# Two projections of a gated MLP as seven products of block sums, in a pass of their own

## The chip, the cores and the metric

The kernel runs on one core of a Trainium2 chip. The metric is the device time of one execution, in microseconds (us), the median of the runs of one kernel. A core has a matrix engine (PE), three engines for elementwise work (DVE, the vector engine; ACT, the activation engine; POOL, GpSimd), and SP, whose queue here issues most DMA transfers. Each engine works through its own queue in order and waits at an instruction whose inputs are not there yet.

## The reference

One encoder layer over 4096 tokens of width 1024, in fp32. All column groups are slices of one projection of the normalised input:

```python
h = rms_norm(x, norm_g[layer])
proj = h @ w_in[layer]
q, k, v, g_att, sg_uv, g_sg, q_mem, g_mem = jnp.split(proj, split_points, axis=-1)
...
uv = jax.nn.gelu(sg_uv)
u, vv = jnp.split(uv, 2, axis=-1)
vv = layer_norm(vv, sg_ln_g[layer], sg_ln_b[layer])
vv = vv.reshape(B, S // SG_CHUNK, SG_CHUNK, N_SG_GROUPS, SG_GROUP_DIM)
mixed = jnp.einsum('gpq,bcqge->bcpge', sg_w[layer], vv)
mixed = mixed + jnp.transpose(sg_b[layer])[None, None, :, :, None]
y_sg = (u * mixed.reshape(B, S, SG_WIDTH)) * jax.nn.silu(g_sg)
```

Here u is columns 2048 to 2559 of the projection, vv 2560 to 3071 and the gate g_sg 3072 to 3583, 512 each. Beside this group stand a dilated attention (q, k, v) and an attention into 256 memory tokens (q_mem, mem); the three results go through one output projection, a residual and a final norm.

## The kernel before

An fp32 product is made of three fp32r matmuls: both factors are split into a high part (a cast on ACT) and the rest (a subtraction on DVE), and high x high, high x low and low x high are summed in PSUM (`mm3`, L194 to L201). One 128 x 1024 by 1024 x 512 product is a group of 8 k-tiles x 3 = 24 matmuls of 128x512.

Raw blocks of 256 KB come from HBM through five buffers (`raw`), for x (`load_x_kt`, L182: cast L185 to `xh`, subtraction L186 to `xl`) and for weights (`load_w_kt`, L165: scaled cast L168 to `wh`, L169 to `wl`, the norm's gain g folded in). Weights lie in three slots of eight pairs: slot 0 in the pool px, slots 1 and 2 in the pool pw. x has ten pairs of buffers, so two k-tiles of the next 512 tokens can be made ready early. The tokens' norm factor rs is not applied to x but to the result (as the scale of an activation, or in a multiplication).

`pass_a` (0 to 575 us) makes v, q and k for eight tiles T of 512 tokens. In its last T it loads vv's weights into slot 0. `pass_b` (575 to 1130 us) makes for each T, in four groups each, vv (slot 0, W[0]), u (slot 1, W[1]) and the gate (slot 2, W[2]). vv passes through Gelu (ACT, L359), statistics, a reciprocal root (POOL, L109) and two scalings (DVE, L361 to L367), and is split again (cast L368, subtraction L369). Then `pm` mixes the positions of a 128-token chunk: 24 matmuls of 128x256 (L392 to L395 call `mm3`), read by L400, which adds a bias and multiplies with u times its gate; L401 stores the result. After pass_b come the memory's keys (L471) and values (L484), q_mem with its gate, the attention and the output projection.

What sets the order: a scheduler places the instructions of each engine by data dependence and estimated times, up to the last T of pass_b; from there on PE, ACT and DVE run in the order in which the code is written (`manual_schedule`, L349).

## Time and profile before

| | us |
|---|---|
| median of three runs | 3117.7 (3115.72 to 3122.05) |
| the profiled execution | 3116.74 |
| its span on the core | 3115.0 |
| PE busy in the span | 3026.7 (97%) |
| pass_b in the trace | 575.27 to 1130.40 |

The span runs from the first to the last instruction of the profiled execution. Busy times of several engines overlap. Matmuls of PE are pipelined: a record lasts about 0.39 us while the next starts 0.23 us after it, so a rate is read from a window and its count. PEclk is the granted clock of PE as a share of its full speed, 2.4 GHz; 0.50 is 1.2 GHz.

### The profile page before, as it was taken

The page shows a single profiled execution, that of the slowest core. Times are in us where ns is not written, and L with a number is a line of the kernel's source. Part 1 is how long each engine was busy: PE and PEld are TensorE (multiplying, and loading weights), DVE is VectorE, ACT ScalarE, POOL GpSimd, SP SyncE. Part 2 cuts the span into 40 slices and gives each one's busy share as a digit, 9 for nine tenths or more (in the row PEclk, how much of TensorE's full clock was granted, in tenths as well). Part 3 has the DMA queues.
Part 4 walks back from the last instruction along what each step waited for, and adds up shares of the span by engine and source line. Part 5 has one row for each costly group of instructions (what it writes and reads, how often), then busy time and mean ns, then how long its engine had stood idle before and what let it go on. Part 6 is the DMA issues. An engine that isn't in the chain of part 4 may idle for free. (4 is left out here: it accounts for less than half of the span.)

```text
span 3115.0 us, 44121 instructions
## 1 busy us (share of the span) xinstructions
PE 3026.7 (97%) x15850; PEld 2526.2 (81%) x15850; DVE 1414.3 (45%) x3669; ACT 1235.0 (40%) x2504; POOL 365.1 (12%) x708
## 2 busy tenths in 40 slices
PE   9999999999999999999999988999999988999998
PEld 7777888888888888888887877888888876888887
DVE  4332323433333355565553345555665564444443
ACT  5213111322222245554553346677766742111111
POOL 1111112000000000000000011122122211111120
PEclk9999999999999999999999999999999998999999
DMA  8558445411211152121127466767777478778773
GB/s 284 189 173 260 155 136 173 145 41 43 66 55 41 36 174 72 51 78 48 51 72 223 152 140 158 147 142 157 158 169 148 106 188 224 200 198 202 207 191 100
DMA packets 344067, 432.47 MB, mean 139 GB/s; under 512 B 154179, under 2 KB 230302, under 8 KB 334630
## 3 DMA queue, kind: packets, MB, share of 16 engines
q1 hardware_dynamic: 325832, 387.26, 45.3%
q0 software_dynamic: 17440, 41.33, 5.2%
q8 instruction: 126, 2.06, 0.3%
q10 hardware_dynamic: 576, 1.05, 0.1%
q14 instruction: 93, 0.76, 0.1%
HBM read 299.27 MB, written 130.21 MB: 138 GB/s over the span
## 5 line engine op out<-in xcount | busy, mean ns | idle before, releaser
L199 PE MATMUL acc<-xh,wh 128*128 128x512 f32 x1192 | 473.6, 398 | 11.1 <-ACT xh L185 11.1
L200 PE MATMUL acc<-xl,wh 128*128 128x512 f32 x1192 | 471.7, 396 | 10.5 <-DVE xl L186 10.3
L201 PE MATMUL acc<-xh,wl 128*128 128x512 f32 x1192 | 470.4, 395 | 0.0
L199 PE MATMUL acc<-wh,xh 128*128 128x512 f32 x1024 | 401.1, 392 | 0.0
L200 PE MATMUL acc<-wl,xh 128*128 128x512 f32 x1024 | 401.0, 392 | 0.0
L201 PE MATMUL acc<-wh,xl 128*128 128x512 f32 x1024 | 400.9, 392 | 0.0
L756 ACT ACTIVATE p<-ring,negm 128x256 f32<-128x256 f32 (+1 forms) x768 | 330.7, 478 | 166.7 <-DVE negm L743 166.7
L667 DVE CUSTOM_DVE_ANT_0 ring<-s,tab 128x256 f32<-128x256 f32 (+1 forms) x768 | 272.3, 392 | 108.9 <-PE s L662 87.7
L200 PEld LDWEIGHTS acc<-xl,wh 128*128 128x128 f32 x1192 | 226.0, 190 | 64.8 <-DVE xl L186 16.8
L199 PEld LDWEIGHTS acc<-xh,wh 128*128 128x128 f32 x1192 | 226.0, 190 | 64.6 <-ACT xh L185 14.9
L201 PEld LDWEIGHTS acc<-xh,wl 128*128 128x128 f32 x1192 | 226.1, 190 | 48.1
L809 PE MATMUL o<-ph,vt 128*65 128x256 f32 (+1 forms) x1280 | 246.5, 340 | 10.7 <-DMA vt<-v 10.7
L662 PE MATMUL s<-khh,qs 128*128 128x256 f32 (+1 forms) x768 | 228.1, 321 | 0.0
L201 PEld LDWEIGHTS acc<-wh,xl 128*128 128x128 f32 x1024 | 191.9, 187 | 43.8
L199 PEld LDWEIGHTS acc<-wh,xh 128*128 128x128 f32 x1024 | 191.9, 187 | 43.4
L200 PEld LDWEIGHTS acc<-wl,xh 128*128 128x128 f32 x1024 | 191.9, 187 | 43.4
L185 ACT CAST xh<-raw 128x512 fp32r<-128x512 f32 x256 | 153.1, 620 | 182.6 <-DMA raw<-in_xT_s 106.5
L809 PEld LDWEIGHTS o<-ph,vt 128*65 128x65 f32 x1280 | 166.5, 139 | 72.5 <-issue 13.5
L825 DVE COPY oacc<-o 65x512 f32<-65x512 f32 x192 | 132.2, 689 | 204.7 <-PE o L809 142.0
L186 DVE TENSOR_TENSOR xl<-raw,xh 128x512 fp32r<-128x512 f32 x256 | 167.6, 687 | 94.8 <-ACT xh L185 93.4
L1133 PE MATMUL acc<-w,aa 128*128 128x512 f32 x768 | 193.3, 401 | 13.5 <-ACT aa L1118 8.3
L662 PE MATMUL s<-kll,qs 128*128 128x256 f32 (+1 forms) x768 | 198.3, 282 | 0.0
(238 smaller groups left out, 4697.0 us busy)
## 6 DMA issues: line engine op xcount, KB each, us to landing
raw<-in_xT_s SPq DMA_DIRECT2D x256, 256.0 KB
og<-oD SPq DMA_DIRECT2D x16, 1536.0 KB
w3k<-wD SPq DMA_DIRECT2D x32, 768.0 KB
oD<-oacc POOLq DMA_DIRECT2D x46, 512.0 KB, 4.7
raw<-in_w_in SPq DMA_DIRECT2D x72, 256.0 KB
xn<-in_x_s SPq DMA_DIRECT2D x32, 512.0 KB
v<-t POOLq DMA_DIRECT2D x128, 128.0 KB, 5.3
khh<-kH SPq DMA_DIRECT2D x32, 512.0 KB
```

Of the source, the lines that this page charges most:

```text
L185: nc.scalar.copy(h[:, :n], raw[:, :n])
L186: nc.vector.tensor_sub(lo[:, :n], raw[:, :n], f(h[:, :n]))
L199: nc.tensor.matmul(out, lh, rh, start=i == 0, stop=False)
L200: nc.tensor.matmul(out, lh, rl, start=False, stop=False)
L201: nc.tensor.matmul(out, ll, rh, start=False, stop=i == n - 1)
L662: nc.tensor.matmul(ps[:, b1, :B["n"]], q, kv, start=i == 0, stop=i == 1)
L667: self.last_dve = nc.vector.tensor_tensor_reduce(out=ring[:, bi, :n], in0=ps[:, b1, :n], in1=e["tab"][:, c, 64 * B["o"]:64 * B["o"] + n], ...
L756: nc.scalar.activation(out, in_, AF.Exp, bias=e["negm"][:, bi:bi + 1], scale=1.0)
L809: nc.tensor.matmul(o[:, o0:o1], vt[:, t, :], pT[:, c0:c1], start=t == 0, stop=t == 4, skip_group_check=True)
L825: nc.vector.tensor_copy(dst, o)
L1133: nc.tensor.matmul(ps, l, w, start=a, stop=o, skip_group_check=True)
```

## The change

u and its gate leave pass_b. A new `pass_u` between pass_a and pass_b treats 256 tokens at a time (16 steps r). With A the 256 x 1024 block of rs times x, cut into four blocks (two token halves of 128, two k halves of 512), and B the 1024 x 1024 weights of u and gate, cut likewise, it forms seven products of 128 x 512 by 512 x 512, 12 matmuls each, in place of eight: A11·B11, S2·T2, S1·T1, S3·T3, A12·B21, A22·T4 and S4·B22. S1 to S4 are sums of blocks of A, T1 to T4 of B. Three PSUM banks per step take them; between products DVE adds the parts that two results share (p1, u2, u3).

- Weights: `split_parts`, called three times in the last T of pass_a, in place of the load of vv's weights, makes T1 to T4, B11, B21 and B22 (40 raw blocks, 12 differences on POOL). B11 and T2 go to slot 0, T1 and T3 to slot 1 (Wq's buffers, free after the last q group), B21 and T4 to slot 2 (Wk's, free after the last k group), B22 into a new pool pz. Vv's weights are loaded in the last step of pass_u.
- `prep(r)`, written one step ahead: one DMA of 1 MB for x (two buffers), the product with rs on POOL (128x2048), four sums on POOL (128x512), seven casts on ACT, seven subtractions on DVE.
- After the products: five adds and two products on DVE, a copy, two Gelu and two Silu on ACT; the 256 x 512 result (u times gate) goes to HBM (`ug`), and pass_b loads it per T (1 MB).
- pass_b: its u and gate groups and their weights' loads are gone; `u` has two buffers; Wmv is loaded one T earlier.

```diff
@@ pass_a, last T
-                    self.Wvv = self.load_w(0, self.w_in(2560), self.g_in)
+                    self.split_parts(0)
...
+                        if T == NT - 1 and cb == 3:
+                            self.split_parts(1 if W is Wq else 2)
...
+    def split_parts(self, rnd):
...
+        def put(name, slot, src, g, kt):
+            pool = (self.px, self.pw, self.pw, self.pz)[slot]
...
+            if g is None:
+                nc.scalar.copy(h, src)
+                nc.vector.tensor_sub(lo, src, f(h))
+            else:
+                nc.scalar.activation(h, src, AF.Copy, scale=g)
+                nc.vector.scalar_tensor_tensor(lo, src, g, f(h), ALU.mult, ALU.subtract)
+
+        def tmp():
+            return self.pz.tile([P, 512], F32, name="wt", tag="wt", bufs=2)
+
+        for kt in range(4):
+            g1, g2 = g_[:, kt:kt + 1], g_[:, kt + 4:kt + 5]
+            b11, b12, b22 = raw(0, 0, kt), raw(0, 1, kt), raw(1, 1, kt)
...
+            if rnd != 1:
+                d, t2 = tmp(), tmp()
+                nc.gpsimd.tensor_sub(d, b12, b11)
+                nc.scalar.activation(d, d, AF.Copy, scale=g1)
+                nc.vector.scalar_tensor_tensor(t2, b22, g2, d, ALU.mult, ALU.subtract)
...
+            else:
+                b21 = raw(1, 0, kt)
+                put("B21", 2, b21, g2, kt)
+                nc.vector.scalar_tensor_tensor(t2, b21, g2, t2, ALU.mult, ALU.subtract)
+                put("T4", 2, t2, None, kt)
+
+    def pass_u(self):
...
+            def prep(r):
...
+                x = p.tile([P, KT, NI], F32, name="xr", bufs=2)
+                nc.sync.dma_start(x, a["xT_s"][:, r * NI:(r + 1) * NI].rearrange("(k p) t -> p k t", p=P))
...
+                nc.gpsimd.tensor_mul(x, x, rs)
+                a11, a12, a21, a22 = [x[:, 4 * j:4 * j + 4, P * i:P * (i + 1)] for i in range(2) for j in range(2)]
+                s1, s2, s3, s4 = [p.tile([P, 4, P], F32, name="s%d" % i, bufs=1) for i in range(4)]
...
+                put("A11", a11)
+                nc.gpsimd.tensor_add(s1, a21, a22)
+                nc.gpsimd.tensor_sub(s2, s1, a11)
+                put("S2", s2)
+                put("S1", s1)
+                nc.gpsimd.tensor_sub(s3, a11, a21)
+                put("S3", s3)
+                put("A12", a12)
+                put("A22", a22)
+                nc.gpsimd.tensor_sub(s4, a12, s2)
+                put("S4", s4)
...
+            for r in range(2 * NT):
...
+                product(b1, "A11", "B11", True)
+                nc.scalar.copy(p1, b1)
+                product(b2, "S2", "T2", True)
+                nc.vector.tensor_add(u2, b2, p1)
+                product(b3, "S1", "T1", True)
+                product(b2, "S3", "T3", False)
+                nc.vector.tensor_add(u3, b2, p1)
+                product(b1, "A12", "B21", False)
+                nc.vector.tensor_add(c22, b3, u3)
+                product(b2, "A22", "T4", False)
+                product(b3, "S4", "B22", False)
+                if r < 2 * NT - 1:
+                    X = prep(r + 1)
+                else:
+                    self.Wvv = self.load_w(0, self.w_in(2560), self.g_in)
+                nc.vector.tensor_add(w[:, 1], b2, p1)
+                nc.vector.tensor_add(c12, b3, u2)
+                nc.scalar.activation(w[:, 0], b1, AF.Gelu_apprx_tanh)
+                nc.scalar.activation(w[:, 1], w[:, 1], AF.Gelu_apprx_tanh)
+                nc.scalar.activation(c22, c22, AF.Silu)
+                nc.scalar.activation(c12, c12, AF.Silu)
+                nc.vector.tensor_mul(w[:, 0], w[:, 0], c12)
+                nc.vector.tensor_mul(w[:, 1], w[:, 1], c22)
+                nc.sync.dma_start(self.ug[r * NI:(r + 1) * NI, :].rearrange("(j p) c -> p j c", p=P), w)
...
@@ pass_b
-                u = p.tile([P, 4, 512], F32, name="u", tag="u")
+                u = p.tile([P, 4, 512], F32, name="u", tag="u", bufs=2)
+                nc.sync.dma_start(u, self.ug[T * TT:(T + 1) * TT, :].rearrange("(j p) c -> p j c", p=P))
...
-                if T == 0:
-                    W[1] = self.load_w(1, self.w_in(2048), self.g_in)
-                    W[2] = self.load_w(2, self.w_in(3072), self.g_in)
-                for j in range(4):
...
-                    self.proj_N(ps, W[1], X, j)
-                    nc.scalar.activation(u[:, j, :], ps, AF.Gelu_apprx_tanh, scale=rs)
-                if T == NT - 1:
+                if T == NT - 2:
                     self.Wmv = self.load_w(1, a["w_kv"][:, 512:1024], self.g_mem)
-                for j in range(4):
...
-                    self.proj_N(ps, W[2], X, j)
-                    t = p.tile([P, 512], F32, name="t", tag="t1", bufs=3)
-                    nc.scalar.activation(t, ps, AF.Silu, scale=rs)
-                    nc.vector.tensor_mul(u[:, j, :], u[:, j, :], t)
```

Three places show how the order of the instructions moves. In all of them a number behind a name is that of the buffer's use. **SP at the end of pass_a**, before: the stores of the last k blocks (kH, kL), the last x block and four of vv's weight blocks.

```order
L308 DMA kH<-qkh 128x512
L309 DMA kL<-qkl 128x512
L182 DMA raw<-in_xT_s 128x512
L165 DMA raw<-in_w_in 128x512 x4
L308 DMA kH<-qkh 128x512
L309 DMA kL<-qkl 128x512
```

The same place of the changed program: L348 loads blocks for the weights' sums, L166 vv's weights, xr is the x of a step, rsb the norm factors.

```order
L348 DMA raw<-in_w_in 128x512
L312 DMA kL<-qkl 128x512
L348 DMA raw<-in_w_in 128x512 x4
L311 DMA kH<-qkh 128x512
L348 DMA raw<-in_w_in 128x512
L312 DMA kL<-qkl 128x512
L166 DMA raw<-in_w_in 128x512 x3
L402 DMA rsb<-rD 128x512
L404 DMA xr<-in_xT_s 128x8x256 x2
```

The x of the first two steps of pass_u stands behind the last blocks for the weights' sums, the last k stores and three blocks of vv's weights. **DVE behind the last k group**, before: the split of that group's result, then vv's weights, between them the statistics of the first vv group.

```order
L217 TENSOR_TENSOR qkl_4295<-t_4292,qkh_4294 128x512
L169 SCALAR_TENSOR_TENSOR wl_4530<-raw_4527,g_in_68,wh_4529 128x512
L169 SCALAR_TENSOR_TENSOR wl_4536<-raw_4533,g_in_68,wh_4535 128x512
L169 SCALAR_TENSOR_TENSOR wl_4542<-raw_4539,g_in_68,wh_4541 128x512
L169 SCALAR_TENSOR_TENSOR wl_4548<-raw_4545,g_in_68,wh_4547 128x512
L169 SCALAR_TENSOR_TENSOR wl_4554<-raw_4551,g_in_68,wh_4553 128x512
L361 BN_STATS st_4398<-t_4396 128x6
```

DVE in the changed program, at the first step of pass_u: L415 splits the blocks (xr_4522, s1_4526 and so on belong to step 0, xr_4656 and s0_4659 to s2_4661 to step 1; the tiles s0 to s3 hold S1 to S4), L447 makes u2 of step 0.

```order
L415 TENSOR_TENSOR xl_4553<-xr_4522,xh_4552 128x512
L415 TENSOR_TENSOR xl_4558<-s3_4528,xh_4557 128x512
L415 TENSOR_TENSOR xl_4664<-xr_4656,xh_4663 128x512
L415 TENSOR_TENSOR xl_4670<-s1_4660,xh_4669 128x512
L415 TENSOR_TENSOR xl_4674<-s0_4659,xh_4673 128x512
L415 TENSOR_TENSOR xl_4679<-s2_4661,xh_4678 128x512
L447 TENSOR_TENSOR u2_4565<-b1_4562,p1_4564 128x512
```

Four subtractions of step 1 stand ahead of u2 of step 0. **PE in the last T of pass_b**, before: the end of the last gate group, then the mixing.

```order
L199 MATMUL acc_8141<-wh_4619,xh_7682 128x512
L200 MATMUL acc_8141<-wl_4620,xh_7682 128x512
L201 MATMUL acc_8141<-wh_4619,xl_7683 128x512
L199 MATMUL pm_8181<-vvh_7686,sgwh_4310 128x256
L200 MATMUL pm_8181<-vvl_7687,sgwh_4310 128x256
```

The same in the changed program: acc_8827 is the last vv group, whose result becomes part of vvh_8706 and vvl_8707.

```order
L200 MATMUL acc_8827<-wh_6859,xh_8702 128x512
L201 MATMUL acc_8827<-wl_6860,xh_8702 128x512
L202 MATMUL acc_8827<-wh_6859,xl_8703 128x512
L200 MATMUL pm_8938<-vvh_8706,sgwh_6883 128x256
L201 MATMUL pm_8938<-vvl_8707,sgwh_6883 128x256
```

Where the u and gate groups stood between vv and the mixing, the mixing now follows its own inputs directly.

## Rows read from the trace of the kernel before

**Rows 1.** The page: busy us, share, instructions; DMA rate in 40 slices of the span.

```profile
PE 3026.7 (97%) x15850; PEld 2526.2 (81%) x15850; DVE 1414.3 (45%) x3669; ACT 1235.0 (40%) x2504; POOL 365.1 (12%) x708
...
GB/s 284 189 173 260 155 136 173 145 41 43 66 55 41 36 174 72 51 78 48 51 72 223 152 140 158 147 142 157 158 169 148 106 188 224 200 198 202 207 191 100
```

**Rows 2.** Windows, PE: length, busy time, matmuls, granted clock, DMA share, GB/s.

```profile
714.04:735.80 21.76, 21.76 (x98) 1.00 0.23 79
735.80:780.62 44.82, 44.82 (x193) 1.00 0.04 12
575.27:1130.40 555.13, 555.13 (x2498) 1.00 0.19 62
```

**Rows 3.** One whole T of pass_b: length, busy PE, PEld, DVE, ACT, POOL, clock.

```profile
714.04:783.43 69.39, 69.39 (x314) 56.73 (x313) 22.92 (x44) 17.32 (x26) 3.67 (x4) 1.00 0.14 46
```

**Rows 4.** Groups by line: shapes, count, busy us, mean ns, idle before.

```profile
L1109 POOL TENSOR_TENSOR og<-og 128x1024 f32<-128x1024 f32 x16 | 38.4, 2403 | 102.4 <-DVE og L1107 102.4
...
L941 POOL TENSOR_TENSOR wqs<-raw,wqs 128x512 fp32r<-128x512 f32 x2 | 2.5, 1271 | 0.0
...
L359 ACT ACT_TABLE_LOAD x8 | 10.3, 1283 | 0.1
```

**Rows 5.** Timeline, DVE and POOL (start, length), and durations of two DVE lines.

```profile
2539.49 2.52 POOL L1109 TENSOR_TENSOR og<-og 128x1024 f32<-128x1024 f32 x1 [31.41 <-DVE og L1107]
...
2539.78 2.78 DVE L947 TENSOR_TENSOR wqs<-raw,wqs 128x512 fp32r<-128x512 f32 x1
...
2542.09 2.72 POOL L1110 TENSOR_TENSOR og<-og 128x1024 f32<-128x1024 f32 x1
2542.48 0.68 DVE L825 COPY oacc<-o 65x512 f32<-65x512 f32 x1
...
L947 DVE TENSOR_TENSOR w<-raw,w x8: 684/691/693, 2560.4 to 2576.7; 128x512 fp32r<-128x512 f32 x8
...
L1082 DVE TENSOR_TENSOR mmA<-io,mmA x16: 679/684/2275, 2543.1 to 3018.0; 128x512 fp32r<-128x512 f32 x16
```

**Rows 6.** Timeline at the end of pass_a: DVE, ACT, SP (its issues).

```profile
573.01 0.45 SPq L182 DMA_DIRECT2D raw<-in_xT_s  x1
...
575.48 0.69 DVE L305 TENSOR_TENSOR t<-acc,rsb 128x512 f32<-128x512 f32 x1 [0.45 <-PE acc L201]
...
576.34 0.62 ACT L185 CAST xh<-raw 128x512 fp32r<-128x512 f32 x1 [2.31 <-DMA raw<-in_xT_s]
...
577.51 0.33 SPq L308 DMA_DIRECT2D kH<-qkh  x1
```

**Rows 7.** A wait of PE in pass_a, and the window behind it.

```profile
311.20 0.80 PE L199 MATMUL acc<-xh,wh 128*128 128x512 f32 x1 [4.75 <-ACT xh L185]
...
311.20:317.64 6.44, 6.44 (x15) 0.50 0.78 235
```

**Rows 8.** Last T of pass_b: vv's chain behind its last matmul; Wmk's last casts.

```profile
1082.79 0.39 PE L199 MATMUL acc<-wh,xh 128*128 128x512 f32 x1
...
1083.05 0.69 ACT L359 ACTIVATE t<-acc,rs_x 128x512 f32<-128x512 f32 x1 [1.12 <-PE acc L201]
...
1086.75 0.62 ACT L368 CAST vvh<-t 128x512 fp32r<-128x512 f32 x1 [3.01 <-DVE t L367]
...
1087.40 0.69 DVE L369 TENSOR_TENSOR vvl<-t,vvh 128x512 fp32r<-128x512 f32 x1 [0.69 <-ACT vvh L368]
...
1093.74 2.06 ACT L168 ACTIVATE wh<-raw,g_mem 128x512 fp32r<-128x512 f32 x3 [0.28 <-DMA raw<-in_w_kv]
```

**Rows 9.** Timeline from the last projection of pass_b to q_mem: PE, SP's issues.

```profile
1127.59 0.28 PE L199 MATMUL pm<-vvh,sgwh 128*128 128x256 f32 x1
...
1134.23 7.19 SPq L165 DMA_DIRECT2D raw<-in_w_in  x6
...
1149.19 7.98 SPq L182 DMA_DIRECT2D raw<-in_xT_s  x8
...
1154.45 0.50 PE L199 MATMUL acc<-xh,wh 128*128 128x512 f32 x1 [0.27 <-ACT xh L185]
```

More of the change, by code (lines that the diff above doesn't have):

```diff
@@ L94, in __init__ @@
         dt("wD", [3, NH, S])
+        dt("ug", [S, 512])
         dt("rowD", [3, NH, RL])
@@ L329, in bcast, with raw @@
         return rsb
+    PAIR = 2048, 3072
+    def split_parts(self, rnd):
+        nc = self.nc
+        if rnd == 0:
+            self.WS = {}
+        g_ = self.g_in
+        def raw(i, j, kt):
+            t = self.px.tile([P, 512], F32, name="raw", tag="raw", bufs=5)
+            nc.sync.dma_start(t, self.a["w_in"][(4 * i + kt) * P:(4 * i + kt + 1) * P, self.PAIR[j]:self.PAIR[j] + 512])
+            return t
+        def put(name, slot, src, g, kt):
+            pool = (self.px, self.pw, self.pw, self.pz)[slot]
+            n = 4 if slot == 3 else 8
+            h = pool.tile([P, 512], F32R, name="wh", tag="wh%d" % slot, bufs=n)
+            lo = pool.tile([P, 512], F32R, name="wl", tag="wl%d" % slot, bufs=n)
+            self.WS[name, kt] = h, lo
+            if g is None:
[9 more added lines that the diff above has]
+            b11, b12, b22 = raw(0, 0, kt), raw(0, 1, kt), raw(1, 1, kt)
+            if rnd == 0:
+                put("B11", 0, b11, g1, kt)
+            if rnd != 1:
[3 more added lines that the diff above has]
+                nc.vector.scalar_tensor_tensor(t2, b22, g2, d, ALU.mult, ALU.subtract)
+            if rnd == 0:
+                put("T2", 0, t2, None, kt)
+                put("B22", 3, b22, g2, kt)
+            elif rnd == 1:
+                d, t3 = tmp(), tmp()
+                nc.gpsimd.tensor_sub(d, b12, b11)
+                put("T1", 1, d, g1, kt)
+                nc.scalar.activation(b12, b12, AF.Copy, scale=g1)
+                nc.vector.scalar_tensor_tensor(t3, b22, g2, b12, ALU.mult, ALU.subtract)
+                put("T3", 1, t3, None, kt)
+            else:
[3 more added lines that the diff above has]
+                put("T4", 2, t2, None, kt)
@@ new lines, in pass_u, with put, product, sb @@
+    def pass_u(self):
+        nc, tc, a = self.nc, self.tc, self.a
+        with tc.tile_pool(name="pu", bufs=1, reuse_waits="tile") as p, tc.tile_pool(name="ppu", bufs=2, space=PSUM, reuse_waits="tile") as pp:
+            rsb = {}
+            def prep(r):
+                if r % 2 == 0:
+                    rsb[0] = p.tile([P, TT], F32, name="rsb", bufs=1)
+                    nc.sync.dma_start(rsb[0], self.rD[:, r * NI:r * NI + TT].broadcast_to([P, TT]))
+                x = p.tile([P, KT, NI], F32, name="xr", bufs=2)
+                nc.sync.dma_start(x, a["xT_s"][:, r * NI:(r + 1) * NI].rearrange("(k p) t -> p k t", p=P))
+                rs = rsb[0][:, r % 2 * NI:(r % 2 + 1) * NI].rearrange("p (o t) -> p o t", o=1).broadcast_to([P, KT, NI])
+                nc.gpsimd.tensor_mul(x, x, rs)
+                a11, a12, a21, a22 = [x[:, 4 * j:4 * j + 4, P * i:P * (i + 1)] for i in range(2) for j in range(2)]
+                s1, s2, s3, s4 = [p.tile([P, 4, P], F32, name="s%d" % i, bufs=1) for i in range(4)]
+                B = {}
+                def put(name, src):
+                    h = self.px.tile([P, TT], F32R, name="xh", tag="xh", bufs=10).rearrange("p (k t) -> p k t", k=4)
+                    lo = self.px.tile([P, TT], F32R, name="xl", tag="xl", bufs=10).rearrange("p (k t) -> p k t", k=4)
+                    nc.scalar.copy(h, src)
+                    nc.vector.tensor_sub(lo, src, f(h))
+                    B[name] = h, lo
+                put("A11", a11)
[9 more added lines that the diff above has]
+                put("S4", s4)
+                return B
+            def product(ps, xn, wn, first):
+                for k in range(4):
+                    (xh, xl), (wh, wl) = X[xn], self.WS[wn, k]
+                    for i, (l, w) in enumerate(((xh, wh), (xh, wl), (xl, wh))):
+                        nc.tensor.matmul(ps, l[:, k, :], w, start=first and k + i == 0, stop=k == 3 and i == 2, skip_group_check=True)
+            def sb(name, bufs=2):
+                return p.tile([P, 512], F32, name=name, bufs=bufs)
+            X = prep(0)
+            for r in range(2 * NT):
+                b1, b2, b3 = [pp.tile([P, 512], F32, name="b%d" % i, bufs=2) for i in range(3)]
+                p1, u2, u3, w = sb("p1", 1), sb("u2", 1), sb("u3", 1), p.tile([P, 2, 512], F32, name="w", bufs=2)
+                c12, c22 = u2, u3
+                product(b1, "A11", "B11", True)
[22 more added lines that the diff above has]
+                nc.sync.dma_start(self.ug[r * NI:(r + 1) * NI, :].rearrange("(j p) c -> p j c", p=P), w)
@@ L336, in pass_b @@
             rsn = self.rs_x
-            raw = p.tile([P, 8, P], F32, name="sgraw", tag="u")
+            raw = p.tile([P, 8, P], F32, name="sgraw")
             nc.sync.dma_start(raw, a["sg_wT"])
@@ L1231, in build @@
             with tc.tile_pool(name="pw", bufs=2, reuse_waits="tile") as b.pw:
-                b.pass_a()
+                with tc.tile_pool(name="pz", bufs=2, reuse_waits="tile") as b.pz:
+                    b.pass_a()
+                    b.pass_u()
                 b.order = ExitStack()
```

4 lines of the change are left out of this document (removed).

## The prediction, made before the changed kernel was run

> **What bounds the kernel now.** I read the page's busy times first: PE is busy for 97% of the span, DVE 45%, ACT 40%, POOL 12% [rows 1]. Then the windows over the second pass (pass_b, from 575.27 to 1130.40 us): PE busy 555.13 of 555.13 us, at granted clock 1.00 [rows 2]. Nothing waits there, so a matmul taken out of it is worth its whole pitch, and any new wait costs its whole length. The pitch is not the mean duration of a record (390 ns, records overlap), but a window divided by its count: the vv groups of one T hold 96 matmuls in 21.76 us, 0.2267 us each; the u and gate groups hold 192 in 44.82 us, 0.2334 us each [rows 2]. One whole T of pass_b takes 69.39 us, with DVE busy for 22.92 and ACT for 17.32 of it [rows 3]: they have much slack now, because vv's chain of vector work hides under the u and gate matmuls.
>
> **What the change removes.** Eight times 44.82 = 358.6 us of matmuls. In their place pass_u has 16 steps r of 84 matmuls (seven products of 12). The two products with weights in slot 0 and the one in the new pool pz I price like vv's groups (slot 0), the four with weights in pw like the u and gate groups (pw): 36 x 0.2267 + 48 x 0.2334 = 19.4 us a step, 309.9 us for 16. Gain 48.7 us; 43.5 (192 x 0.2267) if the pitch differs nowhere, 53.9 if all of pass_u goes at 0.2267. The order of the changed program holds those 84 matmuls a step, so the saving itself is not in doubt.
>
> **What a step asks of the others.** POOL multiplies x by rs (128x2048) and forms four sums (128x512). From 1.27 us for 128x512 and 2.40 for 128x1024 [rows 4], each 512 more cost 1.13, so the product takes about 4.7 and the step 4.7 + 4 x 1.27 = 9.8 us. DVE has 14 operations of 0.69; ACT has seven casts of 0.62, a copy, four Gelu or Silu of 0.69 and two table loads of 1.28 [rows 4, 8]: about 10 us each, a copy counted as a cast. All below 19.4, so by busy time alone no step waits. But the queues are in order, and two engines do not run side by side: in [rows 5] the DVE subtraction at 2539.78 lasted 2.78 us, the others of that line 0.69, and it ended 0.55 after POOL's product (2539.49 + 2.52 = 2542.01). The first of line L1082, at 2543.1, lasted 2.28, where 0.68 is usual, and ended 0.55 after the following POOL product (2542.09 + 2.72 = 2544.81). A DVE operation with both operands in SBUF stood still until POOL's elementwise operation was over; a copy out of PSUM (2542.48) took its usual 0.68 beside POOL, so I let the five adds that read PSUM pass; no row here has an add of that kind there. The Trainium skill, GPSIMD Engine Reference, section 8 (Key points), says that GpSimd shares its SBUF interfaces with VectorE and contends with instructions that have two SBUF inputs; the trace agrees (2.78 against 0.69 us). The page gives no price for that, and it speaks against this change, which puts 9.8 us of POOL work a step beside nine such DVE operations; without any hold the 8 us below and 6 of the boundary would go, and the sum would come to 3128.
>
> **Steps of pass_u in their rhythm.** Turns taken strictly, 9.8 + 9 x 0.55 = 14.8 us a step are less than 19.4. What can be late is the sum u2, for which product S3 waits (it adds onto the same PSUM bank). POOL's long product for the step after holds one DVE subtraction (4.3 us with its own work). Behind it stand, in order, a product, c12 and a subtraction (1.9), a product that waits for the Silu of c12 and then for two of POOL's sums (3.4), a subtraction and u2 (1.2): 10.8 us from a start about 2 us ahead of the step. PE reaches S3 three products of 2.75, 8.2 us, into the step: some 0.5 us late, 8 us for 16 steps. The bounds are 0 and 2.4 a step (a full hold of 4.7 with 0.45 behind it, against the 2.75 of one product), 38 us.
>
> **From pass_a into pass_u.** Here nothing waits today: the last k group is read at 575.48, the last stores go out at 577.51 [rows 6], and from 575.27 PE goes on without a gap [rows 2]. In the changed order SP reaches x of step 0 only behind the last raw blocks for B21 and T4, the k stores and three raws of Wvv (SP's order in the section on the change). T4 and B21 take over Wk's buffers, which the last k group frees only while it runs; with temporaries in pairs, the last two k-tiles each need a POOL difference (1.27), two DVE operations (1.4) and raws behind them (a raw block issued at 573.01 was cast at 576.34, 3.3 us [rows 6]). So with E the end of the k group x is issued at about E + 8 to E + 11. Ahead of it lie some six raws, and the 1 MB itself takes 3.7 us at 284 GB/s [rows 1]: landed near E + 18. POOL's product 4.7, cast 0.62: first matmul at E + 24 (bounds 19 and 40: issue 3 us earlier; the DMA at 200 GB/s, a rate of the later slices). Then S3 waits for u2, which in DVE's order stands behind four subtractions of step 1 (DVE's order there). Those need the rest of POOL's sums for step 0, its whole product for step 1 and three sums more, 4.7 + 7 x 1.27 = 13.6, then casts and DVE operations, 4, and holds of 2 to 3: S3 starts about 20 us after POOL's first product ended, where PE needs 8.9. That is 11 more, and 3 in the step behind. Sum 38; bounds 29 and 55. After such waits the clock falls: behind an idle time of 4.75 us 15 matmuls took 6.44 us at granted clock 0.50 [rows 7], 3.0 more than their 3.4. I count that once (the first cold stretch ends in the wait for u2 anyway): 41 us in all (32 to 58).
>
> **Inside pass_b and at its end.** One T is now vv (21.8) and the mixing pm (2.8), 24.6 us; DVE needs 22.9 - 2.8 = 20.1 of them. The chain from vv's last matmul to pm's inputs is, in [rows 8], from 1082.79 (PE starts the next group) over Gelu at 1083.05 to the cast's end at 1087.37, which pm's first matmul needs, and the last subtraction's at 1088.09 for its second: 4.6 and 5.3 us. The scheduler puts 25 matmuls of the next T ahead of pm (5.7 us), but three subtractions for that T into the chain (+1.8): some 1.2 us late in each of seven T, 8 us (0 to 17). Entering pass_b, T 0 has that and the splitting of the mixing weights: 3 us (0 to 6). In the last T PE runs as written: pm stands directly behind vv (PE's order there), where two projections (44.8 us) lay between. The wait is the bare chain, about 5 us. And what loaded under those projections comes late: mem, Wmk, then 16 blocks of weights and 8 of x, through five buffers. Today raw blocks of weights go out at 1.2 us each (7.19 for 6), x at 1.0 (7.98 for 8) [rows 9]: 16 x 1.2 + 8 = 27 us, behind Wmk's casts (their last ends at 1095.8, 13 us after vv's last matmul [rows 8]; the same instructions). So the first q_mem matmul comes about 40 us after the last vv matmul; today it is 1154.45 - 1127.59 = 26.9 after the last projection [rows 9]. Cost 13 us, pm's wait included (8 to 16). The ug stores and loads (512 KB a step, 1 MB a T) I price at 0: the DMA engines are busy 19% in pass_b [rows 2]; if that cover went, they would show as late x.
>
> **Sum.** 41 + 8 + 3 + 8 + 13 = 73 against 48.7: +24.3 us. The profiled execution (3116.74; its span 3115.0 and 1.7 around it) becomes 3141; it stands 1.0 below the median of the three runs (3117.7), so I forecast 3142.
>
> **Rivals.** (1) Faster: the boundary hides half of itself. SP reaches x by E + 5, it lands by E + 9, the first product starts at E + 15 and u2 comes 5 late: 20 + 3. With no holds in the steps, 0; 0; 3 at the T, 8 at the end: 34 against 48.7, 3103. For it speaks that DMA and SP are idle for long stretches of the last k groups today; against it Wk's buffers, which no earlier issue frees. It decides if x lands before E + 12. (2) No change: no holds in the steps, the boundary at its low end of 32, 4 at the T, 12 at the end: 48 against 48.7, 3117. (3) Much slower: the holds bind every step. DVE's adds out of PSUM queue behind held subtractions, so that POOL's long product falls in full on u2's way each time: 2.4 us a step, 38 instead of 8: 3172. For it speaks that a held operation holds the whole DVE queue; against it the 4.6 us a step that are left over.
>
> **Chances.** The forecast 0.50 (3126 to 3160 by its own terms), faster (1) 0.17, no change (2) 0.15, much slower (3) 0.18. Small terms spread each by about 10 us. About 0.2% (6 us) is what a measurement of this kernel can tell from no change: faster 0.17, same 0.15, slower 0.68. Range 3106 to 3172: half of (1) and half of (3) fall outside.
>
> **What would show it.** Right: a PE gap of 20 us or more at pass_u's start, and one of 7 or more before its S3; in later steps DVE subtractions of 2 to 4 us that end 0.55 after a POOL operation, steps of 19.8 us; pm at 24.6 + 1.2 us a T; a gap of about 5 before the last pm. Wrong: step 0 starting within 12 us of the k group; subtractions of 0.69 beside POOL; steps of 19.0 or of more than 21; the first q_mem matmul less than 32 us after the last vv.

## The result, and the profile after

The changed kernel takes 3137.64 us (median; 3133.94 to 3146.82), the kernel before 3118.53 beside it: ratio 1.0066, 95% interval 1.0047 to 1.0085. It is slower by 0.66%. The forecast was 3142, with a range of 3106 to 3172, and 0.68 on slower. The profiled execution has a span of 3132.2 us against 3115.0.

The page of the changed kernel, busy us, share and instructions, then the DMA rate in 40 slices of the span:

```profile
PE 2985.4 (95%) x15658; PEld 2496.4 (80%) x15658; DVE 1626.9 (52%) x3889; ACT 1343.0 (43%) x2675; POOL 555.6 (18%) x800
...
GB/s 285 185 162 255 174 135 171 192 88 88 88 109 172 174 177 113 48 55 73 48 53 218 167 126 153 150 150 161 164 162 152 105 174 225 212 192 203 208 190 100
```

Against [rows 1] PE lost 41 us of work, while DVE gained 213, ACT 108 and POOL 190, and slices 9 to 14 move 1.3 to 5 times as many bytes. The span grew all the same, so PE must wait where it did not wait before. The windows say where (their first part is the length, then busy us of PE, PEld, DVE, ACT, POOL, then granted clock, DMA share, GB/s): pass_a's end to the first product, step 0, step 1, the other 14 steps, pass_b's vv and pm, and from there to the first q_mem matmul.

```profile
575.81:603.72 27.91, 0.15 (x1) 0.00 (x0) 12.49 (x18) 7.34 (x13) 7.75 (x4) 0.57 0.81 262
603.72:636.90 33.18, 23.63 (x85) 17.93 (x86) 28.35 (x20) 12.99 (x21) 28.00 (x15) 0.84 0.23 72
636.90:657.50 20.60, 19.72 (x86) 15.72 (x85) 17.10 (x15) 9.71 (x15) 13.30 (x6) 1.00 0.27 90
657.50:930.15 272.65, 272.65 (x1178) 220.53 (x1176) 178.48 (x204) 141.13 (x204) 119.97 (x60) 1.00 0.27 87
930.15:1133.41 203.26, 195.95 (x937) 163.21 (x935) 155.65 (x311) 79.32 (x130) 35.58 (x31) 1.00 0.53 172
1133.41:1175.73 42.32, 31.09 (x173) 28.15 (x173) 29.33 (x49) 23.12 (x36) 0.92 (x1) 0.84 0.63 200
```

The fourth window is the part that works: PE is busy without a break in 14 steps, at full clock. From step 3 on a step takes 19.46 us. The waits of PE, of the whole span, name the other parts (us in total, times, longest):

```profile
PE b L434 <- ACT xh L414: 27.8, 1, 27.8
...
PE pm L200 <- ACT vvh L507: 11.8, 8, 4.5
...
PE b L434 <- DVE u L447: 7.0, 2, 6.2
PE acc L608 <- ACT rsb L331: 6.6, 1, 6.6
...
PE b L434 <- DVE xl L415: 3.4, 1, 3.4
```

On PE's timeline (start, length, in brackets the idle time before and who ended it) these are the first matmul of A11·B11, a later one of S2·T2, the first of S3·T3, of the last pm and of the memory's keys, and q_mem, which starts without a wait of its own:

```profile
603.72 0.80 PE L434 MATMUL b<-wh,xh 128*128 128x512 f32 x1 [27.76 <-ACT xh L414]
...
612.39 0.50 PE L434 MATMUL b<-wh,xl 128*128 128x512 f32 x1 [3.37 <-DVE xl L415]
...
623.91 0.77 PE L434 MATMUL b<-wh,xh 128*128 128x512 f32 x1 [6.16 <-DVE u L447]
...
1138.04 0.58 PE L200 MATMUL pm<-vvh,sgwh 128*128 128x256 f32 x1 [4.47 <-ACT vvh L507]
...
1161.92 0.58 PE L608 MATMUL acc<-xh,wh 128*128 128x256 f32 x1 [6.61 <-ACT rsb L331]
...
1175.73 0.39 PE L200 MATMUL acc<-xh,wh 128*128 128x512 f32 x1
```

What leads to the first product is on SP, POOL and DVE. SP issues the last raw blocks of B21 and T4 from 579.28, and x (two loads, steps 0 and 1) only at 589.22; x lands at 598.5, POOL multiplies, ACT casts, PE starts at 603.72 (SP's issues, then POOL, then DVE's last operation on T4):

```profile
579.28 4.34 SPq L348 DMA_DIRECT2D raw<-in_w_in  x4
...
589.22 1.12 SPq L404 DMA_DIRECT2D xr<-in_xT_s  x2
```

```profile
585.98 1.37 POOL L374 TENSOR_TENSOR wt<-raw 128x512 f32<-128x512 f32 x1 [3.67 <-DMA raw<-in_w_in]
598.52 4.49 POOL L406 TENSOR_TENSOR xr<-xr,rsb 128x2048 f32<-128x2048 f32 x1 [11.18 <-DMA xr<-in_xT_s]
...
592.62 0.69 DVE L359 TENSOR_TENSOR wl<-wt,wh 128x512 fp32r<-128x512 f32 x1 [0.74 <-ACT wh L358]
```

### The profile page after: what moved, and what is told of

Read it like the earlier page. It is cut to its first block, busy times and chain, and to the rows that moved or that the text cites. A ratio compares the mean times of both kernels' runs of the same rounds, so it can differ in the third digit from the quotient of the medians.

```text
span 3132.2 us, 44554 instructions
## 1 busy us (share of the span) xinstructions
PE 2985.4 (95%) x15658; PEld 2496.4 (80%) x15658; DVE 1626.9 (52%) x3889; ACT 1343.0 (43%) x2675; POOL 555.6 (18%) x800
## 5 line engine op out<-in xcount | busy, mean ns | idle before, releaser
L434 PE MATMUL b<-wh,xh 128*128 128x512 f32 x448 | 178.2, 398 | 34.8 <-ACT xh L414 27.8
L200 PE MATMUL acc<-wh,xh 128*128 128x512 f32 x512 | 199.7, 390 | 0.0
L202 PE MATMUL acc<-wh,xl 128*128 128x512 f32 x512 | 199.6, 390 | 0.0
L201 PE MATMUL acc<-wl,xh 128*128 128x512 f32 x512 | 199.5, 390 | 0.0
L1257 PEld LDWEIGHTS acc<-w,aa 128*128 128x128 f32 x768 | 146.0, 191 | 50.4 <-ACT aa L1242 10.4
L434 PE MATMUL b<-wh,xl 128*128 128x512 f32 x448 | 177.6, 396 | 3.4 <-DVE xl L415 3.4
```

The source lines that it names most:

```text
L200: nc.tensor.matmul(out, lh, rh, start=i == 0, stop=False)
L201: nc.tensor.matmul(out, lh, rl, start=False, stop=False)
L202: nc.tensor.matmul(out, ll, rh, start=False, stop=i == n - 1)
L434: nc.tensor.matmul(ps, l[:, k, :], w, start=first and k + i == 0, stop=k == 3 and i == 2, skip_group_check=True)
L1257: nc.tensor.matmul(ps, l, w, start=a, stop=o, skip_group_check=True)
```

## The experiments

In each profiled execution I call **the way** the time from the start of pass_a's last matmul to the start of pass_u's last one, less 16 x 19.46 = 311.4 us: what the entry (and any wait in the steps) costs. In the changed kernel it is 929.92 - 575.58 - 311.4 = 42.9 us. e4 leaves the entry as it is in the change, and there the first product comes 1.7 us later and the way is 1.9 us longer; so smaller differences between two traces say nothing. Each group of runs had the kernel before beside it (median 3118.5 to 3120.4), so ratios are the fairer comparison. Two kernels of the table can be told apart by their times from 4 to 9 us on (an estimate: the half widths of both intervals, added in squares). The gain of e1 against the change (0.27%) is just above that; those of e2 against the change, e9 against e5 and e10 against e8 are not, and rest on the traces.

| kernel | first product behind pass_a's last matmul | the way | median us | ratio to before, 95% interval |
|---|---|---|---|---|
| the change | 28.1 | 42.9 | 3137.64 | 1.0066 [1.0047, 1.0085] |
| e1: step 0 early | 0.2 | 32.9 | 3130.32 | 1.0039 [1.0024, 1.0054] |
| e2: product with rs on DVE | 26.2 | 36.9 | 3131.68 | 1.0050 [1.0031, 1.0069] |
| e3: sums made twice | 28.5 | 62.3 | 3160.4 (one run) | |
| e4: Wqm early | 29.8 | 44.8 | 3127.48 | 1.0034 [1.0021, 1.0046] |
| e5: T4 from T2 | 24.8 | 39.2 | 3139.85 | 1.0062 [1.0042, 1.0083] |
| e6: e5 and e1 | 0.2 | 30.1 | 3129.74 | 1.0033 [1.0022, 1.0043] |
| e7: e6 and e4 | 0.2 | 29.8 | 3121.96 | 1.0006 [0.9997, 1.0016] |
| e8: e5, e4 and e2 | 20.7 | 30.7 | 3116.04 | 0.9989 [0.9977, 1.0001] |
| e9: e5, x on POOL's queue | 17.4 | 38.5 | 3131.35 | 1.0041 [1.0026, 1.0056] |
| e10: e8, x on POOL's queue | 14.3 | 24.4 | 3111.23 | 0.9973 [0.9962, 0.9985] |

**The entry: step 0 made early (e1).** The blocks of step 0 (x, the product with rs, the sums and splits) are made in the last T of pass_a, ahead of B21 and T4, by prep0: prep(0) with its x in two tiles (xn) of pass_a.

```diff
                             self.split_parts(1 if W is Wq else 2)
+                            if W is Wq:
+                                self.prep0(p)
...
-            X = prep(0)
+            X = self.X0
```

> Only the entry into pass_u is changed: x of step 0, its product with rs, its four sums and its seven splits are made in the last T of pass_a, behind the weights' sums for slot 1, in buffers that stand idle there; the later steps are as they were. Theory A (the 43 us at the entry are x of step 0 arriving behind the queue of SP, and u2 standing behind the subtractions of step 1): the 27.9 us gap ahead of the first product falls under 3, step 0 lasts 20 to 25 us (33.2 before), some 5 to 8 us are left where step 1 waits for its x; the time falls by some 33 us, 3137.6 to about 3105 (3098 to 3115), below the kernel of before. Theory B (the entry is bound by the weights' sums T4 and B21 or by contention of POOL and DVE, so x early only moves the wait to the fifth and sixth product): the time falls by less than 12 us, above 3125.

Theory A failed: the time fell by 7 us and not by 33. That is B's time, but the wait did not move to the fifth and sixth product, as B had it. PE's first product follows pass_a at once (580.02), and the wait went to S3, the fourth product, in step 0 and again in step 1:

```profile
599.55 0.80 PE L469 MATMUL b<-wh,xh 128*128 128x512 f32 x1 [11.13 <-DVE u L482]
...
637.77 0.77 PE L469 MATMUL b<-wh,xh 128*128 128x512 f32 x1 [12.05 <-DVE u L482]
```

The add that S3 waits for (u) stands in DVE's order behind the rest of the work on T4 and B21 in step 0, and behind step 1's own splits, whose x is issued 17.6 us behind pass_a's last matmul, and four splits of step 2 in step 1. The last of those four lasts 4.98 us, beside POOL's product for step 3. Making the first blocks early moved the queue to the next thing that needs it.

**The entry: a shorter product (e2).** One line, the product with rs on DVE:

```diff
-                nc.gpsimd.tensor_mul(x, x, rs)
+                nc.vector.tensor_mul(x, x, rs)
```

> The product of x with rs (128x2048) goes from POOL to DVE in every step; nothing else changes. DVE then has 2.2 to 2.4 us more a step, POOL 4.6 less. Theory A (POOL's long product holds DVE, but in the steady steps the hold is hidden; only at the entry it lies on the path, twice): DVE's subtractions fall from 1.5 us mean towards 0.8, the steps stay at 19.46, the entry is 4 to 6 us shorter: 3132 to 3134. Theory B (a held DVE costs nothing even at the entry): the entry changes by less than 2 us, 3136 to 3140. If the holds cost the steps after all, they fall under 19.4, which the matmuls alone don't allow.

The way fell by 6.0 us, as theory A has it; the median fell by 6.0 too, but that is within the noise of the two. DVE's subtractions (L415) fall from a mean of 1.34 to 0.90 us, and the steps stay at 19.46. DVE takes 2.29 us for the product in the steps, where POOL takes 4.62 (at the entry 3.36 against 4.49), and no split stands beside it meanwhile: the wait of S3 in step 0 is 3.88 in place of 6.16 us.

**The steps: do POOL and DVE take turns? (e3)** The four sums are made twice on POOL, which adds four sums to POOL's work in a step (some 5 us, at 1.3 each) and nothing else:

```diff
                 nc.gpsimd.tensor_add(s1, a21, a22)
                 nc.gpsimd.tensor_sub(s2, s1, a11)
+                nc.gpsimd.tensor_add(s1, a21, a22)
+                nc.gpsimd.tensor_sub(s2, s1, a11)
...
                 nc.gpsimd.tensor_sub(s3, a11, a21)
+                nc.gpsimd.tensor_sub(s3, a11, a21)
...
                 nc.gpsimd.tensor_sub(s4, a12, s2)
+                nc.gpsimd.tensor_sub(s4, a12, s2)
```

> Each of POOL's four sums of a step is made twice (same values): POOL's work goes from 9.8 to 14.8 us a step. Theory A (POOL and DVE's two-operand work take turns, slack 4.6 us a step): 14.8 + 9 x 0.55 = 19.8 us no longer fit into 19.46, and u2 comes late: steps of 20.5 to 23 us, 17 to 57 us more in all. Theory B (both engines' work only has to fit each by itself, 14.8 and 9.6 against 19.46): steps stay at 19.46, and only the entry grows, by 5 to 8 us.

The steps became 19.93 to 20.01 us in place of 19.46: a step grows, though PE, DVE and ACT have no more work and POOL's 14.8 us would fit, so B's 19.46 is out. A had the direction, but its 20.5 to 23 is too large. POOL's part shows the turns: the sums beside DVE's work last 1.6 to 1.8 us, so that eight sums and the product fill POOL's queue from 701.23 to 718.70 without a break, and ahead of them it waits 2.49 us for a subtraction of DVE. The total is 22.8 us over the change, inside A's 17 to 57, but not for A's reason: of the 19.4 that the way is longer, the steps from r = 3 on have 5.2 and the entry with the first three steps 14.2, where B expected 5 to 8. In the change itself the turns are seen and cost nothing. First DVE, then POOL, in one step of the change:

```profile
700.89 0.69 DVE L465 TENSOR_TENSOR w<-w,u 128x512 f32<-128x512 f32 x1 [1.44 <-ACT u L464]
...
703.21 0.68 DVE L447 TENSOR_TENSOR u<-b,p 128x512 f32<-128x512 f32 x1
...
713.49 0.69 DVE L459 TENSOR_TENSOR w<-b,p 128x512 f32<-128x512 f32 x1 [1.63 <-PE b L434]
714.10 3.00 DVE L415 TENSOR_TENSOR xl<-s,xh 128x512 fp32r<-128x512 f32 x1
...
722.65 0.68 DVE L447 TENSOR_TENSOR u<-b,p 128x512 f32<-128x512 f32 x1
```

```profile
700.96 1.77 POOL L419 TENSOR_TENSOR s<-s,xr 128x512 f32<-128x512 f32 x1
...
703.36 1.29 POOL L422 TENSOR_TENSOR s<-xr 128x512 f32<-128x512 f32 x1 [0.63 <-DVE xl L415]
...
711.92 4.62 POOL L406 TENSOR_TENSOR xr<-xr,rsb 128x2048 f32<-128x2048 f32 x1 [1.31 <-DMA xr<-in_xT_s]
```

The subtraction at 714.10 has both operands in SBUF and lasts 3.00 us; it ends at 717.10, 0.56 after POOL's product (711.92 + 4.62 = 716.54). The adds at 703.21 and 713.49 read PSUM, lie beside POOL too, and take their usual 0.68 and 0.69. That settles what the prediction had only let pass. POOL waits too: its sum at 700.96 lasts 1.77 us, where 1.29 is usual, since DVE's product at 700.89, with both operands in SBUF, began just ahead of it.

Why nothing is late is read from the same rows. POOL's product starts at 711.92, the step (r = 5) at 716.09, 4.2 us later; u is done at 722.65 + 0.68 = 723.33, and S3 starts at 724.35, with 1.0 us in hand. From the product's start to u's end it is 11.41 us. In e3 the same stretch is 754.00 to 765.40, 11.40 us, but the product starts only 2.8 us ahead of the step at 756.80, as soon as POOL is done with its last sum, and S3 waits 0.2 us, in step after step (POOL, DVE, PE):

```profile
754.00 4.62 POOL L406 TENSOR_TENSOR xr<-xr,rsb 128x2048 f32<-128x2048 f32 x1
...
764.72 0.68 DVE L451 TENSOR_TENSOR u<-b,p 128x512 f32<-128x512 f32 x1
...
765.46 0.50 PE L438 MATMUL b<-wh,xh 128*128 128x512 f32 x1 [0.21 <-DVE u L451]
```

The 0.2 is counted from the end of the record before; as records overlap, S3 starts 0.4 us later in the step than without a wait (8.65 against 8.26), and the matmul behind the wait is slower, so the step grows by 0.5.

**The end: Wqm early (e4).** The weights of q_mem are loaded two k-tiles a T in T = 2 to 5 of pass_b, into slot 2, and not behind Wmk in the last T:

```diff
+                if 2 <= T < 6:
+                    if T == 2:
+                        qm = []
+                    qm += [self.load_w_kt(2, self.w_in(3584), self.g_in, 2 * (T - 2) + i) for i in range(2)]
+                    self.Wqm = [x[0] for x in qm], [x[1] for x in qm]
...
-            self.Wqm = self.load_w(2, self.w_in(3584), self.g_in)
```

> Wqm's eight weight blocks (slot 2, free since the end of pass_u) are loaded two in each of T = 2 to 5 of pass_b instead of behind the last T. Theory A (q_mem's first x comes late because 16 weight blocks and mem go through five raw buffers ahead of it): the first q_mem matmul comes about 32 us after the last vv matmul (42.3 before); the time falls by 8 to 10 us, to 3128 to 3130, less up to 3 us that the four T in which DVE has two operations more may lose. Theory B (the end is bound by the mixing standing behind its own inputs and by the mem chain on DVE and ACT): q_mem starts less than 3 us earlier, 3135 to 3139.

Theory A's numbers nearly came: the first q_mem matmul comes 33.6 us after the last vv matmul (1166.98 - 1133.43), in the change 42.6 (1175.73 - 1133.18), and the median falls by 10.2 us. So Wqm's blocks are the cause of 9.0 us, but the path is not only the one that A names. In the change q_mem does not wait for its x. It has been held before, for 6.6 us ahead of the memory's keys, until ACT had copied rsb (a row of factors) out of PSUM; and that copy stands in ACT's order behind casts of Wqm, whose blocks come late. Here is ACT up to the first cast of q_mem's x:

```profile
1159.55 2.07 ACT L169 ACTIVATE wh<-raw,g_in 128x512 fp32r<-128x512 f32 x3 [5.55 <-DMA raw<-in_w_in]
1161.52 0.35 ACT L331 COPY rsb<-acc 128x256 f32<-128x256 f32 x1
...
1173.65 0.60 ACT L186 CAST xh<-raw 128x512 fp32r<-128x512 f32 x1
```

That x is ready at 1174.25, 1.5 us ahead of PE: it would have held q_mem nearly as long. e4 takes both away at once; there q_mem waits for its x (0.39 us), and the keys do not wait. The wait of pm (4.86 from matmul to matmul) stays, as it must: that is the bare chain behind vv.

**The entry: fewer raw blocks (e5, e6, e7).** e5 makes T4 = B21 g - T2 from T2's parts, which already lie in SBUF, so that the last round of block sums loads 4 raw blocks in place of 16 and needs no POOL difference. e6 is this with step 0 early, e7 adds Wqm early.

```diff
-            b11, b12, b22 = raw(0, 0, kt), raw(0, 1, kt), raw(1, 1, kt)
+            if rnd < 2:
+                b11, b12, b22 = raw(0, 0, kt), raw(0, 1, kt), raw(1, 1, kt)
...
-            if rnd != 1:
+            if rnd == 0:
...
-                nc.vector.scalar_tensor_tensor(t2, b21, g2, t2, ALU.mult, ALU.subtract)
-                put("T4", 2, t2, None, kt)
+                h, lo = self.WS["T2", kt]
+                t4 = tmp()
+                nc.vector.scalar_tensor_tensor(t4, b21, g2, f(h), ALU.mult, ALU.subtract)
+                nc.vector.tensor_sub(t4, t4, f(lo))
+                put("T4", 2, t4, None, kt)
```

> The change with one edit: T4 = B21*g - T2 is made from T2's two parts, which already lie in SBUF, so that the last T of pass_a loads 4 raw blocks and not 16 and POOL makes no differences there. Theory A: the way into pass_u (43 us in the change, from the last matmul of pass_a to the steady steps) is set by the weight sums T4 and B21, in whose queue on SP, POOL and DVE x and u stand: without the 12 blocks x is issued some 10 us sooner (the change: 13.4 us behind the last k group), the first product starts 15 to 20 us behind the end of pass_a (27.8 in the change), and the way is 30 to 35 us, the time 3126 to 3130. Theory B: the way is x itself, its load, the product on POOL and the chain of sums and splits: the first product at most 2 us sooner, time 3135 or more.

> The edit of T4 and the early making of step 0's blocks together. Theory A: with step 0's blocks ready, step 0 wants nothing but u2, and u2 stands on DVE behind the rest of the sums for T4 and B21; that rest is short now, so the wait for u2 (11.1 us in step 0 and 12.1 us in step 1 when step 0 alone was early) falls under 4 us each: the way into pass_u is 8 to 18 us, the time 3103 to 3113. Theory B: u2 waits for something else (x of step 1, POOL's products): the waits stay near 11 and 12 us, time about 3130 as with step 0 alone.

> The two edits at the entry and Wqm loaded in T = 2 to 5 of pass_b. Theory A: the entry and the end are apart from each other, their gains add up: 10 us less than with the two entry edits alone, 3093 to 3103, faster than the kernel before by 0.5 to 0.8%. Theory B: the entry stays as with step 0 alone: 3118 to 3122, no difference from the kernel before.

Theory A fell in all three, and B's times came: 3139.85, 3129.74 and 3121.96. Taking 12 of 16 blocks out brought the first product 3.3 us sooner, not 10 (more than B's 2 too). The median of e5 did not fall at all. In its trace pass_u ends 4.0 us sooner, and pass_b loses as much again: pm's waits in seven T are 10.0 us in place of 7.3. But e1, e2 and e9, which have the same pass_b, show 8.8, 9.3 and 8.3 there, so this can be chance; what it is stays open. In e6 S3 of step 0 waits 4.81 us instead of e1's 11.13, which is near A's number. The rest of the waits moved, they did not go: S4·B22 of step 0 now waits 6.59 us for an add that stands behind step 1's first split, and S3 of step 1 waits 12.72 us, since x of step 1 is issued at 596.16 (POOL's row says whom it waits for):

```profile
603.20 4.50 POOL L445 TENSOR_TENSOR xr<-xr,rsb 128x2048 f32<-128x2048 f32 x1 [17.64 <-DMA xr<-in_xT_s]
```

So the blocks of the weight sums are not the cause by themselves. x is late since it is issued late: in SP's order it stands behind the stores of the last k tiles, the last of which (593.00) goes out when DVE has made that tile.

**The three small edits together (e8).** T4 from T2, Wqm early, the product on DVE, step 0 not early (the edits are those shown).

> The edit of T4, Wqm early and the product with rs on DVE, step 0 not made early. Theory A: 10 us from the end, 8 to 12 from T4, 2 to 4 from DVE's product at the entry: 3111 to 3118. Theory B (x's own chain binds): the end gives its 10, the entry 2 to 4 for the product on DVE alone: 3123 to 3126.

3116.04, inside theory A's numbers and below B's: Wqm alone gave 10.2 us in e4, and the way is 12.2 shorter (42.9 to 30.7); the median fell by 21.6. A's shares did not come: T4 gave 3.7 of the way alone (e5) and 6.2 beside DVE's product, not 8 to 12, and that product 6.0, not 2 to 4. The kernel cannot be told from the one before. Its entry shows what is left. With little to do for T4, SP issues x at 584.30 all the same, 8.9 us behind pass_a's last matmul, since the store of the last k tile (kL) stands ahead of it and waits for DVE:

```profile
583.45 0.33 SPq L312 DMA_DIRECT2D kL<-qkl  x1
583.82 0.42 SPq L406 DMA_DIRECT2D rsb<-rD  x1
584.30 1.59 SPq L408 DMA_DIRECT2D xr<-in_xT_s  x2
...
593.08 2.29 DVE L410 TENSOR_TENSOR xr<-xr,rsb 128x2048 f32<-128x2048 f32 x1 [9.66 <-DMA xr<-in_xT_s]
```

**x off SP's queue (e9, e10).** The loads of rsb and x in prep are issued by POOL; e9 has T4 from T2 besides, e10 is e8 with it.

```diff
-                    nc.sync.dma_start(rsb[0], self.rD[:, r * NI:r * NI + TT].broadcast_to([P, TT]))
+                    nc.gpsimd.dma_start(rsb[0], self.rD[:, r * NI:r * NI + TT].broadcast_to([P, TT]))
...
-                nc.sync.dma_start(x, a["xT_s"][:, r * NI:(r + 1) * NI].rearrange("(k p) t -> p k t", p=P))
+                nc.gpsimd.dma_start(x, a["xT_s"][:, r * NI:(r + 1) * NI].rearrange("(k p) t -> p k t", p=P))
```

> T4 from T2's parts, and the loads of rsb and x of pass_u issued by POOL in place of SP, nothing else. With T4 from T2 alone the first product came 24.8 us behind the end of pass_a. Theory C: what holds the entry is x's place in SP's order, behind the last k tiles (kH, kL) and the raw blocks whose buffers come free late; POOL is done with its differences some 6 us ahead of the end of pass_a, so x is issued there, lies in SBUF before DVE is done with T4, and the first product starts 10 to 14 us behind the end; pass_u ends 10 to 14 us sooner than with T4 alone (925.9), the time is 3122 to 3130. Theory D: the entry is set by DVE's own order (the last k tile, T4, then the splits of two steps) and by its turns with POOL: the first product 20 us or more behind the end, the time 3134 or more.

> T4 from T2's parts, Wqm in T = 2 to 5, the product with rs on DVE (these three gave a first product 20.7 us behind the end of pass_a and 3116 us), and now the loads of x and rsb on POOL's queue. Theory C: the first product 10 to 13 us behind the end of pass_a, all else as it was: 3104 to 3109, faster than the kernel before by 0.3 to 0.5%. Theory D: 3113 to 3117, no difference.

e9 lies between its theories. x of step 0 is issued at 565.95, 10 us ahead of pass_a's end, so SP's queue was in the way, as C says. But POOL then stands at the load of step 1's x, whose buffer DVE frees with the last k tile, and multiplies step 0's x only behind that:

```profile
565.95 0.93 POOL L408 DMA_DIRECT2D xr<-in_xT_s  x1
587.26 0.88 POOL L408 DMA_DIRECT2D xr<-in_xT_s  x1 [20.38 <-DVE qkl L218]
588.16 4.51 POOL L410 TENSOR_TENSOR xr<-xr,rsb 128x2048 f32<-128x2048 f32 x1
```

First product 17.4 us behind pass_a, not 10 to 14. And of the 7.4 us gained on e5 there, 6.7 were lost in the steps, of which the middle ones took 19.70 to 19.96 us: with x issued from POOL's own queue its product starts later. So the way is only 0.7 us shorter than e5's; that the median is 8.5 lower, the entry and the steps do not explain. In one such step (POOL, then DVE, then PE):

```profile
725.71 4.64 POOL L410 TENSOR_TENSOR xr<-xr,rsb 128x2048 f32<-128x2048 f32 x1 [2.61 <-DMA xr<-in_xT_s]
...
736.44 0.68 DVE L451 TENSOR_TENSOR u<-b,p 128x512 f32<-128x512 f32 x1
...
737.18 0.50 PE L438 MATMUL b<-wh,xh 128*128 128x512 f32 x1 [0.16 <-DVE u L451]
```

From 725.71 to u's end at 737.12 it is 11.41 us again; the step begins at 728.57, only 2.9 us behind the product's start, and S3 has to wait. Three kernels, one chain of 11.4 us: a start 4.2 us ahead of the step hides it, one of 2.8 or 2.9 does not.

In e10 DVE multiplies, POOL has less to do, and the steps are 19.46 again. Its 3111.23 is 4.8 us under e8: C had 7 to 12 (3104 to 3109), D nothing (3113 to 3117), so the time lies between the two. The trace shows the share of each. SP's place was worth 6.4 us at the first product (20.7 to 14.3 behind pass_a); what is left there is DVE's own order, the last k tile and T4, behind which it takes up x at 587.13. So both C and D name a part, one behind the other. A third part is in neither: the last k tile is itself 3.3 us later than in e8 (DVE starts its split 10.7 us behind pass_a's last matmul, 7.4 in e8). DVE stands 2.9 us for a cast of ACT, and this cast for a store:

```profile
577.74 0.62 ACT L217 CAST qkh<-t 128x512 fp32r<-128x512 f32 x1 [3.62 <-DMA kH<-qkh]
```

In e8 that cast waits for no store. The DMA engines are busy for 0.99 of the time from 570 to 575 us here, 0.49 in e8, so the early x probably delays the k stores; no run tests it. With these four edits the seven products beat the kernel before by 0.27%, with an interval that lies below 1; whether an edit of this kind would also help the kernel before was not tried. The whole of e10's entry, first products and S3 (on PE):

```profile
590.12 0.80 PE L438 MATMUL b<-wh,xh 128*128 128x512 f32 x1 [13.90 <-ACT xh L418]
...
607.09 0.47 PE L438 MATMUL b<-wh,xh 128*128 128x512 f32 x1 [2.30 <-DVE u L451]
```

Against 27.76 and 6.16 in the change: what remains of the way, 24.4 us, is these two waits, one of 1.81 between them, and the slow matmuls behind each.

## Why the prediction was right

The sign and the size held (3142 forecast, 3137.6 measured), and mostly for the reasons given; one term was wrong outright, and the path of another only in part right. That the two times lie within 5 us is in part luck, as the sum below shows.

- **The gain**, 48.7 forecast: 16 x 19.46 = 311.4 us against 358.6, so 47.2. The step was priced at 19.4 from two pitches of [rows 2], and is 19.46: S4·B22, with its weights in pz, runs at 0.2333 us a matmul like the products from pw, not at 0.2267.
- **The entry**, 41 forecast: 42.9. The parts shifted against each other. x was issued 13.4 us behind the end of the k group (589.22 - 575.81), where 8 to 11 were forecast from [rows 6]; the first product came at 27.9, where 24 were. S3 then came 20.9 us after POOL's first product ended (623.91 - 603.01), where 20 were forecast. The 3 for the step behind were too many: its S3 waits 0.9. So the forecast's worked chain over SP, the load, POOL, DVE and S3 was right, the term short by 2 of 43. The gaps forecast as signs of it (20 or more, 7 or more) are 27.8 and 6.2, the second a little less, as 3.4 of the wait already fall in S2·T2.
- **The holds in the steps**, 8 us forecast (0.5 a step): 0 where PE is concerned, the term that failed. The holds are there and have the forecast form (a subtraction of 3.00 us ending 0.56 after POOL's product; [rows 5] had 2.78 and 0.55). The step that failed is the one that put POOL's product "about 2 us ahead of the step": it starts 4.2 ahead, as soon as x lands. That 2 stood on no row. The chain behind it was forecast at 10.8 us and is 11.4. With a start of 2 it would have been late; e9, with 2.8 to 3.1, pays 0.2 to 0.5 a step.
- **Into pass_b and its T boundaries**, 3 + 8 forecast: the eight vv groups and seven pm take 203.26 us; 8 x 21.8 + 7 x 2.8 = 194.0 would be the least, so 9.3. The wait for vvh ([rows 8] has the chain) is 7.3 us in seven T, the 1.2 a T that stood in the sum less a little. The entry has no wait of its own; only pm of the first T waits longer than the others (1.7 us against 0.8 to 1.0).
- **The end**, 13 forecast: the first q_mem matmul comes 42.3 us after the last vv group, 40 forecast; 26.9 before [rows 9], so 15.4. The last pm waits 4.9 between starts (5 forecast). e4 showed the cause of 9.0 us by taking it away: Wqm's loads, as the prediction had it. The path was only half the forecast one. x of q_mem was ready 40.8 us after vv, as forecast, but PE came later still, since the keys had waited 6.6 us for rsb, a wait that the prediction does not have. And the matmuls behind the waits were slower: PE was busy for 31.1 us of this stretch at granted clock 0.84 (the last window above), before for 26.4 at 1.00, which the term left out:

```profile
1127.59:1154.45 26.86, 26.39 (x173) 23.73 (x171) 18.42 (x31) 14.25 (x24) 0.00 (x0) 1.00 0.65 210
```

- **What was not in the sum**: up to q_mem the change is 1175.73 - 1154.45 = 21.3 us late, at the end of the span 17.2. About 4 us come back in the stages behind. That is less than executions of one kernel differ among themselves (12 us for the one before), and its cause is open.

Together: -47.2 + 42.9 + 0 + 9.3 + 15.4 = +20.4, up to q_mem, where the traces have 21.3. The profiled pair differs by 17.2 us at the end, where the sum had 24.3: the 8 for holds were too much, 4 came back in later stages, and the other terms together were 5 too small, so errors of both signs cancelled. Of the rivals, (1) needed x to land before 12 us, (2) an entry of 32; x landed at 22.7 (598.5 - 575.8), and the entry was 42.9. Their other condition, no cost of holds in the steps, came true. (3) needed holds on the way of every step, and a step's 1.0 us in hand says how near that was: e3 and e9 crossed the line, but paid up to 0.5 a step and not 2.4.

## What to carry to other kernels

A pass of its own costs an entry and an exit: when work that was interleaved with other matmuls is pulled apart, follow each queue through the seam, since here 43 us at the entry and 25 behind it ate a saving of 47. Making the first block early, or taking work from one queue, moves such a wait to the next block or the next queue in line (e1, e6, e9); the kernel came below the one before only when several queues were relieved at once (e10). Before a contention is priced into a loop, work out by how much the contended chain leads the engine that bounds: a lead of 4.2 us cost nothing here, one of 2.8 cost 0.5 us a step.

## What the runs showed of the hardware

- DVE operations with both operands in SBUF stand still when POOL's elementwise work has begun, until 0.56 us after it (3.00 us for one of 0.69). Adds that read PSUM are untouched: L447, L452 and L459 of pass_u lie beside POOL in 12 to 14 of their 16 steps and have means of 680 to 691 ns. The turns go both ways: a sum of POOL that begins just behind such a DVE operation lasts 1.77 us and not 1.29. The turn-taking was expected, and the Trainium skill, GPSIMD Engine Reference, section 8 (Key points), names instructions with two SBUF inputs as the ones that contend; these rows agree, and add the price. That the chain through it is so regular I had not expected: 11.40 to 11.41 us in a step of each of three kernels.
- The product of 128x2048 elements takes POOL 4.5 to 4.6 us and DVE 2.29 in the steps (3.36 beside POOL's sums, at e2's entry), so DVE did it in half the time, and moving it to the engine that looked busier (DVE 52%, POOL 18%) shortened the way by 6 us.
